# A hybrid attention and RWKV-7 block on one core: the tile scheduler orders instructions by its timeline simulation

## The chip, the cores and the metric

The kernel runs on one core of a Trainium2 chip. The metric is device time in microseconds (us), from the start to the end of one execution. The engines are named as in the profile: PE is TensorE (matmuls, with PEld its weight loads), DVE is VectorE, ACT is ScalarE, POOL is GpSimd, SP is SyncE, which issues the DMAs. "Profiled execution" is one run taken with the hardware profiler.

## The reference

One layer for 1024 tokens of width 1024, in float32. The parts that matter here, cut:

```python
h = rmsnorm(x, g_mix)
z = h @ w_in                       # columns: MLA latents | RWKV r,k,v,decay,a,g | two gates of 1024
o_mla  = mla_branch(z[MLA], ...)   # 8 heads, causal attention, blocks of 128 queries
o_rwkv = rwkv7_branch(z[RWKV], ...)
#   S_t = S_{t-1} diag(decay_t) + (S_{t-1} a_t) b_t^T + v_t k_t^T ;  y_t = S_t r_t
#   then a norm per head, bonus, output gate, @ w_o_rwkv
mix = sigmoid(gate0) * o_mla + sigmoid(gate1) * o_rwkv
x = x + mix @ w_out
hid = square(relu(rmsnorm(x, g_ffn) @ w_ffn_up))     # 1024 -> 4096
x = x + hid @ w_ffn_down                             # 4096 -> 1024
# then the gated per-layer embedding (ple) and the final rmsnorm
```

## The kernel before, in words

Activations are kept with the 1024 channels on partitions (eight tiles of 128) and the 1024 tokens along the free axis. Every dense product is written with its operands split in a high and a low part of type fp32r: `split_act` makes the high part as a cast on ACT and the low part as a difference on DVE (L318/L319 for activations, L215/L216 for weights), and three products are summed in a PSUM tile `psd` (L225: `xh*wh`, `xl*wh`, `xh*wl`), 48 matmuls of 128x512 for a block of 128 output channels.

The work around the change, in the order of the program:

- **Projections of the input** (`main`, a generator over all blocks of `w_in`): first the RWKV and MLA columns, then the two gates, 16 blocks. The gate blocks aren't needed before the merge, and the program uses them as filler: `weave` alternates the generator with other generators, one step of each in proportion to constants (`T_MAIN`, `T_EARLY`, `T_LATE`).
- **The RWKV recurrence in chunks of 64 tokens** (`recurrence`): 16 steps `chain(ci)`, a pair of steps for each group of 128 tokens. In each step PE, DVE and ACT alternate: products with the state `W` (L795, tile `pc`; L801, tile `py`), a copy `qs` (L797, DVE), a product with an inverse made earlier (L806), two copies into `W` (L807 DVE, L808 ACT), the products for the next state (L812) and the output (L820), the new state (L816, DVE), then the statistics of the output (L825 to L830). Two products are independent of the state: `vT` (L778) and `bk` (L784). `pre(g)` (L712 to L756) prepares the next group beside it, and `finish(g)` (L836 to L857) ends a group: a norm, transposes `yT` (L846), ACT and DVE operations and two stores. The last group's `finish`, behind the loop, is called the tail here.
- **Attention** (L1049 to L1100), by heads and blocks of 128 queries, beside projections of the latents (`qp`, `kn`, `v`).
- **Merge and output projection**, with the residual `res` (L1203).
- **The norm ahead of the FFN** (`row_sums_rstd`, L1207): column sums of squares on PE (L288, tile `st`), a short run of DVE operations, a scaled identity `dg` (L1215, DVE), its product with ones (L1220, tile `rb`, PE), a copy (L1221, ACT), and the scaling of `res` by `rb` (L1361, DVE). Beside it runs a product that nothing needs until the end: the ple projection, eight blocks of 12 matmuls (L1564).
- **FFN** in a Strassen-like form (L1338, tiles `psX`, `psY`, `psZ`), with operands `xb` and `sw` split on ACT and DVE (L318, L319) from `res` and its sums `bt` (L1385 to L1418).

The program runs under a tile framework. The code only gives each instruction, its operands and its place in the program; the framework's scheduler then chooses, from the instructions whose operands are ready, the order in which each engine's instructions are written, and puts in the semaphore waits. To choose, it needs a time for each candidate, and this comes from a model inside the framework. Each engine of the chip runs its list in the order so written.

## Time and profile before

| | before |
|---|---|
| median of 3 runs | 1784.69 us (1783.11 to 1784.8) |
| profiled execution | 1785.7 us, of which 1783.6 us span |
| mean granted PE clock | 0.991 of full speed |
| PE busy | 1730.2 us, 97% of the span |
| weight loads (PEld) busy | 1398.0 us, 78% |
| DVE busy | 1198.3 us, 67% |
| ACT busy | 834.8 us, 47% |
| POOL busy | 261.1 us, 15% |

The span runs from the first to the last instruction of the profiled execution. An engine's busy time is the time that its instructions took; times of PE and PEld overlap, since weights are loaded ahead. A granted clock of 1.00 is TensorE's higher level, 2.4 GHz, and 0.50 is 1.2 GHz.

### The profile page before, as it was taken

How to read it: one execution, taken by the hardware profiler on the slowest of the kernel's cores; microseconds unless marked ns; L12 is line 12 of the kernel's file. 1: busy time of each engine (PE TensorE's matmuls, PEld its weight loads, DVE VectorE, ACT ScalarE, POOL GpSimd, SP SyncE). 2: the span in 40 equal slices, each digit the busy share in tenths (PEclk: the TensorE clock that was granted, in tenths of full speed). 3: DMA queues.
4: the chain of work that ended last, by engine and by line, in shares of the span. 5: the costliest groups of instructions: out<-in, count | busy, mean ns of one | idle time of the engine just before them, and what ended most of it. 6: DMA issues, size and time to landing. Idle time of an engine off the chain costs nothing.

```text
span 1783.6 us, 26948 instructions
## 1 busy us (share of the span) xinstructions
PE 1730.2 (97%) x10525; PEld 1398.0 (78%) x10525; DVE 1198.3 (67%) x1882; ACT 834.8 (47%) x1409; POOL 261.1 (15%) x206
## 2 busy tenths in 40 slices
PE   7999999899999999999999999999999999999997
PEld 6877877777787867776887887888888888888886
DVE  6546695857777678888364369555668787787665
ACT  5553333234444365565344156555557344354444
POOL 2000000000000021212000203232323333332000
PEclk9999999999999999999999999999999999999999
DMA  6257674744543510014443334544558754451402
GB/s 196 71 204 215 195 204 113 188 131 120 155 123 101 182 44 24 24 60 155 140 121 128 95 142 131 166 141 143 166 176 260 243 169 149 154 182 48 154 13 95
DMA packets 245694, 246.13 MB, mean 138 GB/s; under 512 B 48729, under 2 KB 194752, under 8 KB 245568
## 3 DMA queue, kind: packets, MB, share of 16 engines
q1 hardware_dynamic: 243792, 239.65, 43.9%
q0 software_dynamic: 1760, 4.76, 0.8%
q8 instruction: 83, 1.36, 0.3%
q14 instruction: 43, 0.35, 0.1%
q10 hardware_dynamic: 16, 0.00, 0.0%
HBM read 162.31 MB, written 81.54 MB: 137 GB/s over the span
## 4 chain that ended last, share of the span: by engine, by line
PE 56%; DVE 5%; ACT 2%; issue 1%; POOL 0%; DMA 0%; DVEq 0%; ACTq 0%; POOLq 0%
PE psX L1338 18%; PE psd L225 12%; PE psY L1338 9%; PE psZ L1338 5%; PE po L1100 3%; PE pb L234 2%; PE pT L1087 1%; PE qp L234 1%; PE s L1057 1%; PE s L1059 1%; PE s L1058 1%; DVE xb L319 1%; DVE res L1361 1%; PE xT L1175 0%; DVE sw L319 0%
## 5 line engine op out<-in xcount | busy, mean ns | idle before, releaser
L1338 PE MATMUL psX<-xb,sw 128*128 128x512 f32 x768 | 177.4, 389 | 2.3 <-ACT hid L1441 1.2
L1338 PE MATMUL psX<-hb,sw 128*128 128x512 f32 x768 | 176.8, 389 | 0.0
L225 PE MATMUL psd<-xh,wh 128*128 128x512 f32 x528 | 172.8, 404 | 0.0
L225 PE MATMUL psd<-xl,wh 128*128 128x512 f32 x528 | 171.3, 402 | 0.0
L1338 PEld LDWEIGHTS psX<-xb,sw 128*128 128x128 f32 x768 | 144.0, 188 | 32.9 <-ACT hid L1441 1.6
L1338 PEld LDWEIGHTS psX<-hb,sw 128*128 128x128 f32 x768 | 144.2, 188 | 29.9
L225 PE MATMUL psd<-xh,wl 128*128 128x512 f32 x528 | 137.4, 399 | 0.0
L319 DVE TENSOR_TENSOR sw<-sw,sw 128x512 fp32r<-128x512 f32 x128 | 95.1, 747 | 58.2 <-ACT sw L318 58.0
L215 ACT CAST wh<-wr 128x1024 fp32r<-128x1024 f32 (+2 forms) x72 | 62.4, 869 | 152.3 <-PE psd L225 137.3
L318 ACT CAST sw<-sw 128x512 fp32r<-128x512 f32 x128 | 79.4, 620 | 102.1 <-PE psX L1338 37.0
L225 PEld LDWEIGHTS psd<-xh,wh 128*128 128x128 f32 x528 | 99.9, 192 | 22.3 <-issue 0.7
L225 PEld LDWEIGHTS psd<-xl,wh 128*128 128x128 f32 x528 | 100.0, 191 | 22.0
L225 PEld LDWEIGHTS psd<-xh,wl 128*128 128x128 f32 x528 | 97.3, 188 | 21.2
L216 DVE TENSOR_TENSOR wl<-wr,wh 128x1024 fp32r<-128x1024 f32 (+2 forms) x72 | 71.7, 997 | 60.9 <-PE psd L225 42.8
L318 ACT CAST sw<-wr 128x512 fp32r<-128x512 f32 x96 | 59.3, 622 | 71.5 <-PE psX L1338 39.3
L1338 PE MATMUL psY<-hb,sw 128*128 128x512 f32 x384 | 89.6, 389 | 0.0
L1338 PE MATMUL psY<-xb,sw 128*128 128x512 f32 x384 | 89.6, 389 | 0.0
L319 DVE TENSOR_TENSOR sw<-wr,sw 128x512 fp32r<-128x512 f32 x96 | 81.1, 845 | 12.6 <-ACT sw L318 12.4
L1338 PEld LDWEIGHTS psY<-hb,sw 128*128 128x128 f32 x384 | 72.1, 188 | 14.9
L1338 PEld LDWEIGHTS psY<-xb,sw 128*128 128x128 f32 x384 | 72.1, 188 | 14.9
L318 ACT CAST hb<-braw 128x1024 fp32r<-128x1024 f32 x56 | 58.7, 1048 | 52.2 <-DMA braw<-hid_d 20.1
L319 DVE TENSOR_TENSOR hb<-braw,hb 128x1024 fp32r<-128x1024 f32 x56 | 76.3, 1362 | 9.4 <-ACT hb L318 9.1
(409 smaller groups left out, 3546.8 us busy)
## 6 DMA issues: line engine op xcount, KB each, us to landing
hid_d<-hid SPq DMA_DIRECT2D x112, 256.0 KB, 4.3
braw<-hid_d SPq DMA_DIRECT2D x56, 512.0 KB, 4.4
wr<-in_w_in_dram SPq DMA_DIRECT2D x35, 512.0 KB, 5.3
wr<-in_w_ffn_up_dram SPq DMA_DIRECT2D x32, 512.0 KB, 5.0
wr<-in_w_ffn_down_dram SPq DMA_DIRECT2D x32, 512.0 KB, 4.3
gate_d<-gt SPq DMA_DIRECT2D x16, 512.0 KB, 3.7
gate<-gate_d SPq DMA_DIRECT2D x16, 512.0 KB, 3.7
xt<-in_x_dram SPq DMA_DIRECT2D x8, 512.0 KB, 8.4
```

The costliest lines, as they stand in the source:

```text
L215: A.copy(dst(wh), src)
L216: V.tensor_tensor(dst(wl), src, dst(wh).bitcast(F32), ALU.subtract)
L225: T.matmul(acc[:, h, :], lhsT=wt[:, k, :], rhs=r[k][:, h * 512:h * 512 + 512], start=wt is wh and k == 0 and ri == 0, stop=wt is wl and k ...
L234: T.matmul(acc, lhsT=wt[:, k, :], rhs=r[k][:, sl], start=wt is wh and k == 0 and ri == 0, stop=wt is wl and k == kb - 1)
L318: A.copy(hi, src)
L319: V.tensor_tensor(lo, src, hi.bitcast(F32), ALU.subtract)
L1057: T.matmul(sc[:, pi, :wc], lhsT=qh_[0:96, qs], rhs=kh_[0:96, ks], start=True, stop=False)
L1058: T.matmul(sc[:, pi, :wc], lhsT=qh_[0:96, qs], rhs=kl_[0:96, ks], start=False, stop=False)
L1059: T.matmul(sc[:, pi, :wc], lhsT=ql_[0:96, qs], rhs=kh_[0:96, ks], start=False, stop=not lastp)
L1087: T.transpose(out=tp_[:, b * P:(b + 1) * P], in_=prs[i][:, (4 * g + b) * P:(4 * g + b + 1) * P], identity=ident)
L1100: T.matmul(po[i * 64:i * 64 + 64, 0:P], lhsT=vt[kb // 2][:, kb % 2, h * 64:h * 64 + 64], rhs=pts[i][:, kb * P:(kb + 1) * P], start=kb == 0 ...
L1338: T.matmul(acc, lhsT=w[:, wl_, j, :], rhs=part(b, xl_, j), start=start and s == 0, stop=key == LAST[bank] and s == len(steps) - 1, skip_gr ...
```

## The change

The context in which the scheduler works is opened with another option. With `schedule_with_timeline_sim=True` the scheduler times candidate instructions with its timeline simulation in place of its default timing. Nothing else of the program is edited: the instructions, their shapes and their number on each engine are the same in both, and only their order (and with it the waits) differs.

```diff
-    with _tile.TileContext(nc) as tc:
+    with _tile.TileContext(nc, schedule_with_timeline_sim=True) as tc:
         tile_block(tc, *args)
```

The order on PE differs in many places. Three are shown. In all of them a name such as `psd_651_4674` is one tile, and `x8` stands for eight like instructions in a row.

**The recurrence on PE.** In the list of before, counted from the first L795 of one step to the first L795 of the next, the stretches ahead of step 0, between the steps and behind the start of step 15 hold these numbers of L225 matmuls: 1080 ahead of step 0, then 1, 7, 41, 0, 50, 0, 50, 0, 51, 0, 50, 0, 50, 0, 11 between the steps, and 1201 behind the start of step 15. With the change they are 1168 ahead, then 37, 35, 43, 40, 43, 36, 43, 41, 2, 0, 0, 0, 0, 0, 0, and 1104 behind. Step 10, the tile `pc_665`, is one of those that lose their filler; the list of PE before, from its first L795 on (`psd_651` is a gate block):

```order
L795 MATMUL pc_665_4767<-W_655_4716,q3_619_4471 64x64
L225 MATMUL psd_651_4674<-xh_11_165,wl_650_4671 128x512
L795 MATMUL pc_665_4767<-W_655_4716,q3_619_4471 64x64 x7
L225 MATMUL psd_651_4674<-xh_11_165,wl_650_4671 128x512
L225 MATMUL psd_651_4674<-xh_12_166,wl_650_4671 128x512
L801 MATMUL py_666_4768<-W_655_4716,q3_619_4471 64x64 x8
L806 MATMUL pc_665_4767<-qs_667_4777,mt1_1198 64x64 x8
L225 MATMUL psd_651_4674<-xh_12_166,wl_650_4671 128x512
L225 MATMUL psd_651_4674<-xh_13_167,wl_650_4671 128x512 x2
L225 MATMUL psd_651_4674<-xh_14_168,wl_650_4671 128x512 x2
L225 MATMUL psd_651_4674<-xh_15_169,wl_650_4671 128x512
L820 MATMUL py_666_4768<-W_655_4716,ar_637_4601 64x64
```

The same step with the change:

```order
L795 MATMUL pc_665_4767<-W_655_4716,q3_619_4471 64x64 x8
L736 MATMUL bo_677_4857<-r_671_4794,blkr_1192 128x128 x4
L806 MATMUL pc_665_4767<-qs_667_4777,mt1_1198 64x64 x8
L801 MATMUL py_666_4768<-W_655_4716,q3_619_4471 64x64 x8
L820 MATMUL py_666_4768<-W_655_4716,ar_637_4601 64x64
L812 MATMUL pc_665_4767<-W_655_4716,bk_663_4762 64x64 x8
L820 MATMUL py_666_4768<-W_655_4716,ar_637_4601 64x64 x7
L846 MATMUL yT_686_4894<-ident_92,yc_605_4415 64x64 x16
L752 MATMUL sc_692_4929<-q3_673_4796,sh_674_4797 128x128 x4
L801 MATMUL py_699_4971<-W_676_4840,q3_619_4471 64x64 x8
```

The dense matmuls between L795 and L806, and between L806 and L820, have gone; the blocks they belong to now stand ahead of step 9. The gate blocks that stood beside the last steps and the tail (`psd_752`, `psd_799`, `psd_809`) stand there too, and only `psd_837` and `psd_844` are still behind the transposes of the tail, `yT_810`.

**The norm ahead of the FFN on PE.** The list of before, around the column sums (`st`) and the product for `rb`:

```order
L288 MATMUL st_1687_9776<-ones_131,ssq_1650_9353 128x1 x8
L1564 MATMUL psd_1704_9839<-pl_1632_9250,pwh_1641_9286 128x512
...
L1564 MATMUL psd_1706_9855<-ph_1631_9249,pwl_1645_9293 128x512
L1220 MATMUL rb_1692_9797<-dg_1691_9795,ones_131 128x512
L1220 MATMUL rb_1693_9800<-dg_1691_9795,ones_131 128x512
```

With the change:

```order
L288 MATMUL st_1687_9776<-ones_131,ssq_1650_9353 128x1 x8
L1564 MATMUL psd_1708_9871<-ph_1630_9248,pwh_1641_9286 128x512 x2
...
L1564 MATMUL psd_1712_9903<-ph_1630_9248,pwl_1642_9287 128x512
L1220 MATMUL rb_1692_9797<-dg_1691_9795,ones_131 128x512
L1220 MATMUL rb_1693_9800<-dg_1691_9795,ones_131 128x512
```

Of the 96 matmuls of the ple projection, 17 stood ahead of the column sums before, and 36 do with the change; 35 stood ahead of the product for `rb`, and 69 do with the change.

**The first operands of the FFN on DVE.** Before, the scalings of `res` (L1361) alternate with the low parts of the first operands (L319, `xb`):

```order
L1361 SCALAR_TENSOR_TENSOR res_1502_8536<-res_1502_8536,pc_rest_134,rb_1686_9775 128x1024
L1361 SCALAR_TENSOR_TENSOR res_1504_8538<-res_1504_8538,pc_rest_134,rb_1686_9775 128x1024
L319 TENSOR_TENSOR xb_1720_9957<-res_1502_8536,xb_1718_9955 128x512
L1361 SCALAR_TENSOR_TENSOR res_1506_8540<-res_1506_8540,pc_rest_134,rb_1686_9775 128x1024
L319 TENSOR_TENSOR xb_1720_9957<-res_1504_8538,xb_1718_9955 128x512
```

With the change:

```order
L1361 SCALAR_TENSOR_TENSOR res_1502_8536<-res_1502_8536,pc_rest_134,rb_1686_9775 128x1024
L1361 SCALAR_TENSOR_TENSOR res_1504_8538<-res_1504_8538,pc_rest_134,rb_1686_9775 128x1024
L1361 SCALAR_TENSOR_TENSOR res_1506_8540<-res_1506_8540,pc_rest_134,rb_1686_9775 128x1024
...
L1361 SCALAR_TENSOR_TENSOR res_1509_8543<-res_1509_8543,pc_rest_134,rb_1686_9775 128x1024
L1385 TENSOR_TENSOR bt_1729_9984<-res_1502_8536 128x512
L319 TENSOR_TENSOR xb_1720_9957<-res_1502_8536,xb_1718_9955 128x512
```

All eight scalings now stand ahead of the first low part, where two did.

Elsewhere: the projections inside attention (`kn`, `qp`) are written some blocks earlier, with the same numbers of matmuls for each head; the two inverses made for the recurrence have 42 (first) and 83 (second) fewer dense matmuls ahead of the first product of their last stage (L684), and about 42 between each of the following pairs of products, where 1 to 3 stood for most; the FFN's list differs by swaps of neighbours; the last stage's is the same.

## Rows read from the trace of the kernel before

**Rows 1.** The page, busy time of each engine, share of the span, instructions

```profile
PE 1730.2 (97%) x10525; PEld 1398.0 (78%) x10525; DVE 1198.3 (67%) x1882; ACT 834.8 (47%) x1409; POOL 261.1 (15%) x206
```

**Rows 2.** By stretch: length, busy PE PEld DVE ACT POOL (instructions), PE clock, DMA share, GB/s

```profile
388.20:576.90 188.70, 188.34 (x2317) 149.66 (x2316) 142.05 (x332) 81.18 (x158) 0.00 (x0) 1.00 0.49 131
576.90:603.60 26.70, 26.70 (x195) 21.42 (x195) 11.83 (x24) 9.40 (x16) 0.00 (x0) 1.00 0.45 137
...
647.00:853.00 206.00, 197.07 (x1383) 147.03 (x1382) 167.44 (x382) 120.72 (x307) 40.92 (x36) 1.00 0.19 65
...
1063.50:1107.00 43.50, 41.25 (x181) 33.52 (x179) 41.97 (x52) 28.53 (x46) 12.52 (x7) 1.00 0.31 98
1107.00:1670.00 563.00, 562.99 (x2484) 466.33 (x2485) 387.80 (x484) 278.47 (x432) 173.85 (x112) 1.00 0.52 164
```

**Rows 3.** Waits of PE: line waited for, total us, times, longest

```profile
PE xT L376 <- DVE xt L370: 8.0, 2, 6.8
PE y L684 <- DVE x L677: 6.2, 1, 6.2
...
PE rT L293 <- DVE rr L207: 3.1, 1, 3.1
...
PE L L640 <- DVE a L632: 2.2, 2, 1.3
```

**Rows 4.** Stretches in the recurrence, and behind two gaps of PE

```profile
388.20:403.40 15.20, 15.12 (x235) 12.21 (x234) 12.70 (x31) 5.25 (x13) 0.00 (x0) 1.00 0.64 171
506.28:511.74 5.46, 5.46 (x102) 4.78 (x101) 3.59 (x9) 2.01 (x5) 0.00 (x0) 1.00 1.00 284
506.28:533.94 27.66, 27.66 (x324) 21.99 (x323) 20.48 (x47) 12.49 (x24) 0.00 (x0) 1.00 0.55 145
237.50:244.20 6.70, 6.70 (x43) 4.93 (x44) 6.67 (x9) 0.74 (x2) 0.00 (x0) 0.50 0.23 54
353.40:360.20 6.80, 3.14 (x11) 2.50 (x12) 2.47 (x2) 2.99 (x3) 0.00 (x0) 0.50 0.92 175
```

**Rows 5.** Two of these stretches and the tail, the dense matmuls of L225 alone

```profile
388.20:403.40 15.20, 2.92 (x8) 1.32 (x8) 1.00 0.64 171
506.28:533.94 27.66, 13.92 (x50) 8.84 (x50) 1.00 0.55 145
576.85:603.58 26.73, 23.30 (x98) 18.08 (x98) 1.00 0.45 137
```

**Rows 6.** Critical chain, around the output projection: start, us, piece

```profile
955.45 82.10 PE psd L225 x362
```

**Rows 7.** Timeline of step 15 and the tail: start, us, instruction

```profile
576.85 0.75 PE L795 MATMUL pc<-W,q 128*64 128x64 f32 x16
...
578.07 1.23 DVE L216 TENSOR_TENSOR wl<-wr,wh 128x1024 fp32r<-128x1024 f32 x1
...
586.77 0.69 DVE L839 TENSOR_TENSOR yc<-yc,rr 128x512 f32<-128x512 f32 x1
...
593.30 1.15 PE L846 MATMUL yT<-ident,yc 64*64 64x64 f32 x32
...
603.58 0.62 PE L225 MATMUL psd<-xh,wh 128*128 128x512 f32 x2
```

**Rows 8.** Timeline around the norm ahead of the FFN

```profile
1037.38 1.07 PE L1564 MATMUL psd<-ph,pwh 128*128 128x512 f32 x4
...
1041.91 1.95 PE L288 MATMUL st<-ones,ssq 128*128 128x1 f32 x16 [0.52 <-DVE ssq L313]
...
1047.93 1.88 PE L1220 MATMUL rb<-dg,ones 128*128 128x512 f32 x4
...
1050.46 2.48 DVE L1361 SCALAR_TENSOR_TENSOR res<-res,pc_rest,rb 128x1024 f32<-128x1024 f32 x2 [3.86 <-ACT rb L1221]
...
1052.86 0.68 DVE L319 TENSOR_TENSOR xb<-res,xb 128x512 fp32r<-128x512 f32 x1
...
1063.50 2.88 PE L1338 MATMUL psX<-xb,sw 128*128 128x512 f32 x12
```

## The prediction

> **What bounds the kernel now.** I read the page first, then busy times by stretch, the waits of PE, and the timeline in three places. PE works 1730.2 of 1783.6 us [rows 1], so only 53.4 us are idle, and a new order can win no more than that plus what a low clock costs; it can lose much more, by taking cover from a chain of dependent work. By stretch [rows 2] the reader is to see which engine stands behind PE. In the FFN (1107 to 1670) PE is busy 562.99 of 563.00 us: no order of neighbours changes that. In the recurrence (388.2 to 576.9) PE is also full, 188.34 of 188.70, but with a mixture: by the counts of the order 311 dense matmuls lie between its steps, and 98 more beside the tail [rows 5]. Between the norm and the full FFN (1063.5 to 1107) DVE is the nearest to full, 41.97 of 43.5 us. Attention has some slack on all engines. The waits of PE [rows 3] are few and early: 8.0 us for the first transposes, 6.2 for the second inverse, 3.1 and 2.2 for the norms of the recurrence. The only stretches at the low clock that matter lie behind two of these waits [rows 4], the two stretches at 0.50.
>
> **The change, part by part.** Instructions and durations stay; a dense matmul that moves from one full stretch of PE to another is free. So I price only the places that lose or gain cover.
>
> *A. The recurrence.* The order takes away the 151 dense matmuls that stood between steps 8 and 14, the 11 ahead of step 15, and those beside the tail up to `psd_837`. What was covered is read from one pair of steps: 27.66 us from step 9 to step 11, of which 50 matmuls are dense [rows 4, 5]. A dense matmul takes 82.10/362 = 0.2268 us on PE when they follow each other [rows 6]; so dense work is 11.3 us of the pair, and PE's own work there 27.66 - 11.3 = 16.3 us. If PE bounded a bare pair, it would take 16.3 us and the move would be free. It won't: DVE works 20.48 us in the pair, of which one weight split of 1.23 us (L216) [rows 7] belongs to the dense block, which leaves 19.3 us. So 19.3 is the lower bound of a bare pair. Three rows say that DVE won't reach it: in the half without dense work, 506.28 to 511.74, DVE is busy 3.59 of 5.46 us, 1.87 idle, and two such dependent halves give 19.3 + 2 x 1.87 = 23.0; the first pair, with only 8 dense matmuls, has DVE busy 12.70 of 15.20, 84%, and 19.3/0.84 is 23.0 again [rows 4]. The steps are a dependent chain through three engines, but with the order free of dense rows DVE can run `pre` and `finish` in the holes; I take 22. Each bare pair then costs 22 - 16.3 = 5.7 us over the free case, three pairs 17 us (bounds 9 from 19.3, 20 from 23.0). Step 14 has 11 dense matmuls and no `pre` beside it; I put its loss at nothing, between 0 and the 2.5 us that they take.
>
> The tail: from the L795 of step 15 at 576.85 to the next block `psd_837` at 603.58 [rows 7] are 26.73 us, with 98 dense matmuls = 22.2 us [rows 5], so 4.5 us are PE's own. The chain in it ends on DVE at 586.77 + 0.69 = 587.46, 10.6 us after the L795; the transposes could have run then, but stood behind a dense block until 593.30. With the cover gone ahead of step 9, the tail costs 10.6 + 1.15 = 11.8 us before PE has dense work again, against 4.5: +7.3. Bounds: 5, if the DVE work that goes with the dense blocks (1.23 us twice) delayed the chain before, and 8. **A = 17 + 7 = +24 us** (14 to 30).
>
> *B. The norm ahead of the FFN.* 34 more matmuls of the ple projection stand ahead of the product for `rb` (69 against 35): 34 x 0.2268 = 7.7 us later on PE. It ran at 1047.93 [rows 8], so now at about 1055.6. The scaling on DVE waits for it (it began at 1050.46), and from there to 1107 DVE is the bound (96% of the stretch behind 1063.5), so what it starts later it ends later. Then eight scalings of 1.24 us stand ahead of the first low part in place of two, which delays the first FFN product: 1050.46 + 7.7 + 8 x 1.24 + 0.69 + 0.68 = 1069.5 against 1063.50, with PE idle in between, for the ple projection is used up by 1063.5. This lies inside the delay of DVE's list, so it isn't added. **B = +8 us**; from 3, if PE's own 41.25 us in the stretch show that DVE's list had reserve, to 10.
>
> *C. The inverses.* Fewer dense matmuls stand ahead of their last stage, so the waits of 3.1 and 6.2 us stay or grow; against that, about 42 stand between the products that ran nearly bare, part of it at clock 0.50. If all three waits went, 6.2 + 3.1 + 2.2 = 11.5 us, and the two slow stretches (6.70 and 3.14 us of PE at half speed, 4.9 us to win). I take the two as about equal: **C = +2** (-10 to +12; the upper end is 42 x 0.2268 = 9.5 us less cover, plus the next wait).
>
> *D. The start.* A weight split and a statistic stand ahead of the first two activations on DVE; one such split is 1.23 us [rows 7]. The first transposes come about 2 us later, the later ones earlier. **D = +1** (-2 to +4).
>
> *E. Attention, merge, FFN.* In attention PE is busy 197.07 of 206.00 us [rows 2], 8.9 idle, and the same filler is written a block earlier. Nothing at 0 (-4 to +6); the FFN is full on PE and its list nearly the same, 0.
>
> Sum: 24 + 8 + 2 + 1 = **+35** on the profiled execution's 1785.7, 1820.7 us; the median shown is 1.0 us lower than the profiled execution, so **1819.5 us**.
>
> **The rivals.** *The clock falls in the bare steps.* With 22 us for 16.3 of PE, PE waits some 3 us in each step, in pieces. Behind a single wait of 3.1 and one of 6.2 us the granted clock was 0.50 for 6.7 and 6.8 us [rows 3, 4]. Against it: in attention PE idles 8.9 us in many pieces and the clock stays at 1.00 [rows 2], and the first pair, nearly bare, has 1.00 [rows 4]. The price: PE's own work from step 8 to the tail is 3 x 16.3 + about 13 + 4.5 = 66 us; at half speed throughout 132, against some 91 available, so +41; for most of it +30, and the time is about **1850**. In the Trainium skill ("TensorE: Matmul & The Clock Gate", Part 1: The HAM clock gate) the throttled state is the default, and it is activity that releases it; by that rule the bare steps are the ones at risk, and the two rows at 0.50 agree with it, while the attention row shows that short pieces of idleness don't suffice. I leave this case one chance in ten.
>
> *Not slower: the filler was worth more early than late.* The 88 dense matmuls that now stand ahead of step 0 lie where PE waited, and the bare steps fill PE by themselves. For it: in the first pair PE was busy 15.12 of 15.20 us with 8 dense matmuls [rows 4]. Against it: that pair has no `finish` beside it, and DVE has 19.3 us in a later one. Price: the early waits and slow stretches give 11.5 + 4.9 = 16.4 us, the pairs cost nothing, the tail 7 and B at its lower bound 3: 1785.7 + 10 - 16.4 - 1.0 = about **1778**. It decides from the point where a bare pair takes under about 17 us.
>
> *Only the norm and the tail cost.* Pairs at DVE's 19.3, or early gains of about 10 us: 1785.7 + 9 + 7 + 5 - 8 - 1 = about **1798**, mildly slower.
>
> *Nothing measurable.* The order differs almost everywhere, so "no change" could come only as a balance of the above, within about 3.6 us.
>
> **How the numbers follow.** A difference of 0.2%, 3.6 us, is about what a measurement of this kernel can tell from no change. Chances: the forecast, slower by 20 to 50 us, 0.60; mildly slower (4 to 20 us), 0.17; clock in the bare steps, 0.10; balance, 0.06; faster, 0.07. So slower 0.87, same 0.06, faster 0.07. The likeliest is 1819.5. The range from 1796 to 1845 takes in the mildly slower case from its middle on and the bounds of the sum (A 14, B 3, C 0, D 0 give 1802; A 30, B 10, C 12, D 4 give 1841), and leaves out the balance, the faster case and most of the case of the clock.
>
> **What would show it.** In the trace of the changed kernel: (A) pairs of steps from step 8 on at 21 to 23 us with DVE busy over 85% and PE under 80%, the early pairs at 33 us or more with PE full, and about 12 us from the last L795 to `psd_837`; (B) `rb` about 8 us later relative to the first ple matmul, a hole of 5 us or more on PE ahead of the first `psX`, and the FFN full from about 8 us later; (C) waits of PE at L684 and L293 as long as before or longer. A shows wrong if the bare pairs run at 17 us with PE full, or at a clock of 0.50; B, if PE fills before DVE's list is through; the whole, if the early stretches give back over 15 us.

## The result: 4.45% slower, outside the forecast range

| | before | with the change |
|---|---|---|
| median | 1783.9 us (1781.41 to 1784.8, 4 runs) | 1863.33 us (1862.19 to 1867.39, 4 runs) |
| profiled execution, span | 1785.7, 1783.6 us | 1863.51, 1861.8 us |
| mean granted PE clock | 0.991 | 0.963 |
| PE idle in the span | 53.4 us | 108.3 us |

The ratio is 1.0445 (95% interval 1.043 to 1.0459). The sign was forecast; the size wasn't: +35 us forecast, +79 measured. The page of the changed kernel shows where to look; these are the row of busy times [rows 1] and two of the rows by slices of 1/40 of the span (46.5 us each):

```profile
PE 1753.5 (94%) x10525; PEld 1431.6 (77%) x10525; DVE 1208.9 (65%) x1882; ACT 834.0 (45%) x1409; POOL 260.6 (14%) x206
...
PE   5999999999997778998899998999999999999998
...
PEclk9999999899996699999999999999999999999998
```

PE's idle time has doubled (1861.8 - 1753.5 = 108.3 us), and PE is busy 23 us longer with the same instructions, because part of them ran at a lower clock: the 13th and 14th slice (558 to 652 us), 7 tenths busy, stand at 6 tenths of the clock. This is the second half of the recurrence.

To put the loss in its places I compare when the same matmul starts in both traces, and take off what only changed sides: a dense matmul more ahead of it counts 0.2268 us [rows 6]. What is left is called the net delay; the last column is its growth from the row above. The product of step 0, for instance, starts 28.9 us later but has 88 dense matmuls more ahead of it (1168 against 1080), so its net delay is 28.9 - 88 x 0.2268 = 9.0 us.

| first matmul of | before, us (dense ahead) | after, us (dense ahead) | net delay | forecast for the piece | measured |
|---|---|---|---|---|---|
| transposes, L376 | 9.7 (0) | 13.7 (0) | 4.0 | D +1 | +4.0 |
| step 0, L795 | 388.2 (1080) | 417.1 (1168) | 9.0 | C +2 | +5.0 |
| step 9 | 506.3 (1280) | 562.9 (1488) | 9.5 | A 0 | +0.5 |
| step 15 | 576.9 (1391) | 649.8 (1488) | 50.9 | A +17 | +41.4 |
| last `yT`, L846 | 593.3 (1448) | 659.2 (1488) | 56.8 | A +7 | +5.9 |
| first scores, L1057 | 646.3 (1584) | 712.5 (1584) | 66.2 | none | +9.4 |
| merge, L1175 | 851.1 | 921.8 | 70.8 | E 0 | +4.6 |
| `rb`, L1220 (34 ple matmuls more ahead) | 1047.9 | 1123.4 | 67.8 | | -3.0 |
| 13th `psX`, L1338 | 1066.2 | 1141.3 | 75.1 | B +8 | +7.3 |
| last transposes, L1637 | 1760.2 | 1838.6 | 78.5 | 0 | +3.4 |

More than half is one piece, steps 9 to 15. The steps there and a filled one ahead of them, by stretch from one step's first product to the next (columns as in [rows 2]):

```profile
501.67:518.82 17.15, 17.15 (x165) 13.64 (x164) 10.99 (x22) 6.33 (x12) 0.00 (x0) 1.00 0.45 124
562.93:575.04 12.11, 6.79 (x121) 5.63 (x121) 8.48 (x21) 5.92 (x12) 0.00 (x0) 0.89 0.98 237
575.04:596.77 21.73, 16.87 (x172) 14.59 (x172) 14.87 (x35) 5.55 (x12) 0.00 (x0) 0.50 0.08 23
596.77:612.26 15.49, 11.86 (x109) 10.22 (x109) 9.09 (x17) 4.91 (x9) 0.00 (x0) 0.50 0.53 142
612.26:628.46 16.20, 11.66 (x164) 10.01 (x164) 11.08 (x30) 5.55 (x12) 0.00 (x0) 0.71 0.11 30
628.46:637.58 9.12, 8.69 (x102) 7.75 (x101) 3.39 (x9) 2.18 (x5) 0.00 (x0) 0.52 0.23 65
637.58:649.75 12.17, 7.75 (x148) 6.73 (x148) 8.78 (x25) 4.04 (x12) 0.00 (x0) 0.86 0.01 2
```

The first row is a filled step: PE full at 1.00. Then the filler is gone (the next two rows are the pair that took 27.66 us before with 50 dense matmuls [rows 4]; now 12.11 + 21.73 = 33.8 us with none), and the granted clock is 0.50 to 0.89. The same steps 9 to 15 in one row, before and with the change:

```profile
506.28:576.85 70.57, 70.29 (x904) 55.86 (x903) 52.42 (x127) 31.03 (x62) 0.00 (x0) 1.00 0.47 124
562.93:649.75 86.82, 63.63 (x812) 54.93 (x812) 55.69 (x134) 28.15 (x62) 0.00 (x0) 0.65 0.30 77
```

Before, 111 of the matmuls are dense, 25.2 us by the price above, so PE's own work was 45.1 us. With the change there are none, and PE is busy 63.6 us: 18.5 us more, of which about 1 us is work that changed sides (812 matmuls against 904 - 111 = 793). PE waits 23.2 us where it waited 0.3. So the 41.4 us are about 18 us of the same work at a lower clock and 23 us of waits.

The clock fell here, in the timeline around step 9 (start, us, instruction, idle ahead of it and its releaser):

```profile
566.76 0.65 SPq L716 DMA_DIRECT2D r<-rkv_d  x1
...
573.43 0.69 DVE L732 TENSOR_TENSOR q<-r,e 128x512 f32<-128x512 f32 x1 [2.21 <-DMA r<-rkv_d]
574.04 0.85 DVE L816 TENSOR_TENSOR W<-pc,dt 64x256 f32<-64x256 f32 x2
...
575.04 1.12 PE L795 MATMUL pc<-W,q 128*64 128x64 f32 x16 [3.69 <-DVE W L816]
```

The state update (L816), for which the next step's product waits, stands on DVE behind the preparation of the next group (L732), and that waits 2.21 us for its load of `r`, issued at 566.76. PE waits 3.69 us in one piece; before it PE had worked in pieces, 6.79 us of the 12.11 in the step; from here on the rows show 0.50.

The tail and what follows, in the same view:

```profile
649.75 0.69 PE L795 MATMUL pc<-W,q 128*64 128x64 f32 x16
...
659.18 1.97 PE L846 MATMUL yT<-ident,yc 64*64 64x64 f32 x32 [4.95 <-DVE yc L839]
...
661.08 1.22 PE L225 MATMUL psd<-xh,wh 128*128 128x512 f32 x2
...
712.50 0.28 PE L1057 MATMUL s<-kh,q 96*128 96x256 f32 x1
```

From the last step's product to the next dense matmul are 11.3 us (11.8 forecast). But from the last `yT` to the first scores are 53.3 us, and before they were 646.3 - 593.3 = 53.0, although 136 dense matmuls lay in them before (1584 - 1448) and now 96. Before, and with the change:

```profile
593.30:646.29 52.99, 50.38 (x247) 41.05 (x247) 39.41 (x50) 27.53 (x45) 7.57 (x8) 1.00 0.52 161
659.18:712.50 53.32, 46.50 (x207) 37.19 (x207) 37.82 (x48) 26.02 (x44) 7.73 (x8) 0.89 0.42 135
```

Without the 40 dense matmuls (9.1 us) PE had 50.4 - 9.1 = 41.3 us of work here. It took 46.5 at a clock of 0.89, 5.2 us more, and PE waits 6.8 us in place of 2.6, 4.2 more: together the 9.4 us of the table. In the other runs below the same stretch is 52.3 to 54.8 us, with 96 to 136 dense matmuls in it.

Around the norm [rows 8]:

```profile
1114.14 1.84 PE L288 MATMUL st<-ones,ssq 128*128 128x1 f32 x16
...
1123.41 1.88 PE L1220 MATMUL rb<-dg,ones 128*128 128x512 f32 x4
...
1125.95 9.66 DVE L1361 SCALAR_TENSOR_TENSOR res<-res,pc_rest,rb 128x1024 f32<-128x1024 f32 x8 [6.78 <-ACT rb L1221]
...
1131.28 0.61 PE L1338 MATMUL psX<-xb,sw 128*128 128x512 f32 x2
...
1136.13 0.68 DVE L319 TENSOR_TENSOR xb<-res,xb 128x512 fp32r<-128x512 f32 x1
...
1136.87 3.78 PE L1338 MATMUL psX<-xb,sw 128*128 128x512 f32 x8 [4.97 <-DVE xb L319]
```

PE has nothing ready from 1131.9 to 1136.87 (two products of `psX` ran on the high parts, the third needs the low part that stands behind eight scalings of 9.66 us in all). The long waits of PE over the whole execution [rows 3]:

```profile
PE xT L376 <- DVE xt L370: 11.1, 1, 11.1
PE yT L846 <- DVE yc L839: 8.2, 3, 5.0
PE y L684 <- DVE x L677: 6.2, 3, 4.6
...
PE st L288 <- DVE ssq L539: 3.6, 1, 3.6
...
PE psd L225 <- DVE pg L1594: 1.9, 1, 1.9
```

The start waits 11.1 us where it waited 8.0; the inverse waits 6.2 in three pieces; a wait for a sum of squares (L539, ahead of the recurrence) of 3.6 us is new; and one of 1.9 us in the last stage.

### The profile page after: what moved, and what is told of

It reads as the page before. It is cut to its first block, busy times and chain, and to the rows that moved or that the text cites. A ratio compares the mean times of both kernels' runs of the same rounds, so it can differ in the third digit from the quotient of the medians.

```text
span 1861.8 us, 27023 instructions
## 1 busy us (share of the span) xinstructions
PE 1753.5 (94%) x10525; PEld 1431.6 (77%) x10525; DVE 1208.9 (65%) x1882; ACT 834.0 (45%) x1409; POOL 260.6 (14%) x206
## 4 chain that ended last, share of the span: by engine, by line
PE 56%; DVE 6%; ACT 2%; issue 1%; DMA 1%; DVEq 0%; ACTq 0%; SPq 0%
PE psX L1338 18%; PE psd L225 12%; PE psY L1338 9%; PE psZ L1338 5%; PE pb L234 2%; PE po L1100 2%; PE qp L234 1%; PE pT L1087 1%; DVE nmx L1063 1%; PE psd L1564 1%; PE s L1057 1%; PE s L1059 1%; PE s L1058 1%; DMA latf<-lat_d 1%; DVE prob L1070 1%
## 5 line engine op out<-in xcount | busy, mean ns | idle before, releaser
L1338 PE MATMUL psX<-xb,sw 128*128 128x512 f32 x768 | 181.6, 393 | 5.9 <-DVE xb L319 5.2
L1338 PE MATMUL psX<-hb,sw 128*128 128x512 f32 x768 | 180.3, 389 | 0.0
L1338 PEld LDWEIGHTS psX<-xb,sw 128*128 128x128 f32 x768 | 145.5, 190 | 37.5 <-DVE xb L319 6.1
L225 PE MATMUL psd<-xh,wh 128*128 128x512 f32 x528 | 171.8, 405 | 0.0
L225 PE MATMUL psd<-xl,wh 128*128 128x512 f32 x528 | 171.2, 402 | 0.0
L1338 PEld LDWEIGHTS psX<-hb,sw 128*128 128x128 f32 x768 | 144.1, 188 | 29.9
L225 PE MATMUL psd<-xh,wl 128*128 128x512 f32 x528 | 135.2, 401 | 0.0
L319 DVE TENSOR_TENSOR sw<-sw,sw 128x512 fp32r<-128x512 f32 x128 | 96.1, 752 | 55.8 <-ACT sw L318 55.6
L225 PEld LDWEIGHTS psd<-xl,wh 128*128 128x128 f32 x528 | 101.1, 193 | 22.4
L225 PEld LDWEIGHTS psd<-xh,wh 128*128 128x128 f32 x528 | 100.8, 194 | 21.9 <-issue 0.4
L225 PEld LDWEIGHTS psd<-xh,wl 128*128 128x128 f32 x528 | 99.0, 191 | 21.8
L319 DVE TENSOR_TENSOR sw<-wr,sw 128x512 fp32r<-128x512 f32 x96 | 91.8, 967 | 12.4 <-ACT sw L318 11.0
L1338 PE MATMUL psY<-hb,sw 128*128 128x512 f32 x384 | 92.7, 389 | 0.0
L1338 PE MATMUL psY<-xb,sw 128*128 128x512 f32 x384 | 91.5, 390 | 0.0
L1338 PEld LDWEIGHTS psY<-xb,sw 128*128 128x128 f32 x384 | 72.4, 188 | 15.1
L1502 DVE TENSOR_TENSOR res<-psX,res 128x512 f32<-128x512 f32 x64 | 44.0, 688 | 60.9 <-PE psX L1338 59.0
L1338 PEld LDWEIGHTS psY<-hb,sw 128*128 128x128 f32 x384 | 72.1, 188 | 15.0
```

What stands on the lines that cost most here:

```text
L225: T.matmul(acc[:, h, :], lhsT=wt[:, k, :], rhs=r[k][:, h * 512:h * 512 + 512], start=wt is wh and k == 0 and ri == 0, stop=wt is wl and k ...
L319: V.tensor_tensor(lo, src, hi.bitcast(F32), ALU.subtract)
L1338: T.matmul(acc, lhsT=w[:, wl_, j, :], rhs=part(b, xl_, j), start=start and s == 0, stop=key == LAST[bank] and s == len(steps) - 1, skip_gr ...
L1502: V.tensor_tensor(dst, acc, dst, ALU.add)
```

## The experiments

All ratios are to the kernel before, run on the same chip beside the experiment. The theory after the result: the filler that left the last steps is the cause, and it costs twice, by the chain's own latency at full clock (which the forecast had) and by the low clock that the bare steps bring about. Two rivals: the option's fine order on DVE is needed for the loss (the load wait above); or the low clock only goes along with latencies that would be there anyway. In most of the kernels edges hold an instruction behind another on the same engine in the order that is written, with no wait: `behind(ins, key)` below, where `mark[key]` is the earlier one.

**1. Option on, filler held back.**

```diff
-  T.matmul(acc[:, h, :], lhsT=wt[:, k, :], ...)                 # L225, dense
+  behind(T.matmul(acc[:, h, :], lhsT=wt[:, k, :], ...), "step")
-  T.matmul(pc_[LOH[h], 0, j, :], ...)                           # L795 of a step
+  mark["step"] = T.matmul(pc_[LOH[h], 0, j, :], ...)
```

> The option stays on, and each dense matmul (L225) of the recurrence's stretch is written behind the first product (L795) of the step that the program traces ahead of it, so 16 to 32 of them lie in every gap between steps. If the pulled-forward filler is the cause (A), the 41 us lost between steps 9 and 15, the 6 of the tail and the 9 up to the first scores go: about 1863 - 56 = 1807 us, clock near 1.00 through the recurrence. Rival: the loss lies in the fine order of the steps themselves (DVE's list, the transposes), which stays: 1835 or more.

Measured 1836.86 us, ratio 1.0304 (1.0285 to 1.0323): 26.5 us back, of the 56 expected. The net delay grows from 13.4 at step 0 to 33.0 at step 15, evenly, in place of 9.0 to 50.9. In the steps, 19.6 us are left of 41.9, so holding the filler back wins more than half of the loss there and a third of the whole, and the rival's bound of 1835 is met: something else costs some 20 us in the steps. Two of them, of 12.13 and 17.52 us:

```profile
491.19:503.32 12.13, 11.76 (x135) 9.12 (x135) 9.38 (x20) 5.97 (x12) 0.00 (x0) 1.00 0.96 283
503.32:520.84 17.52, 17.20 (x205) 13.99 (x205) 12.86 (x32) 6.82 (x14) 0.00 (x0) 1.00 0.01 4
```

PE is nearly full, and the clock is 1.00 in these two; in the next two (520.84 to 554.98) it is 0.92 and 0.88. What the 20 us are, run 6 tells apart in part.

**2. Option off, filler forward.** The mirror image: the program of before, with the gate blocks handed out early.

```diff
-  run(weave([(recurrence(), T_LATE), (main, T_MAIN)], lead=True))
+  run(until(main, 19)); run(weave([(recurrence(), T_LATE), (until(main, 75), 800)]))
```

> The option is off, as before, but the program hands out the gate blocks of the recurrence early, so that steps 7 to 15 stand bare (3 dense matmuls in all). If bare steps by themselves cost the time (low clock included), this is slower than before by 40 to 55 us: 1825 to 1840. Rival: the option's order of DVE, in which the preparation of the next group stands ahead of the state update and waits for its loads, is needed for the loss; then about +20 at a clock of 1.00: 1800 to 1808.

Measured 1843.17 us, ratio 1.0343 (1.0326 to 1.036), 61 us slower than before and 3 us above the upper end of the first expectation. Net delays: -4.0 at step 8, 39.6 at step 15 (43.6 us in the bare steps), 45.2 at the last `yT`, 55.7 at the first scores, and nothing behind it (55.3 at the end). So a loss of A's size appears without the option and without its order on DVE. Over steps 9 to 15 alone (559.70 to 638.48), this run is busy on PE for 63.55 of 78.78 us, as long as the changed kernel (63.63), and waits 15.2 us where that waits 23.2: the longer PE work is the same without the option, and 8 us of waits go with the option's order. From step 6 to step 12 of it:

```profile
511.18:532.44 21.26, 21.26 (x219) 16.45 (x218) 17.00 (x39) 10.92 (x20) 0.00 (x0) 1.00 0.39 99
532.44:537.90 5.46, 5.46 (x101) 4.78 (x100) 3.58 (x9) 1.40 (x4) 0.00 (x0) 1.00 1.07 302
537.90:559.70 21.80, 14.46 (x173) 12.34 (x172) 16.16 (x38) 8.00 (x17) 0.00 (x0) 0.67 0.31 68
559.70:570.12 10.42, 10.42 (x104) 8.94 (x105) 5.08 (x13) 2.35 (x6) 0.00 (x0) 0.55 0.72 200
570.12:589.34 19.22, 12.59 (x169) 11.12 (x168) 14.36 (x34) 7.95 (x17) 0.00 (x0) 0.74 0.15 44
589.34:600.22 10.88, 10.88 (x104) 9.35 (x105) 5.51 (x14) 2.56 (x6) 0.00 (x0) 0.51 0.78 215
```

The first row is filled, the second the short half behind it, without dense matmuls, at a clock of 1.00: 5.46 us. The third is the first bare long half, PE busy 14.46 of 21.80, and the clock falls within it. From there each short half takes 10.4 to 10.9 us, with PE full, in place of 5.46: at half the clock twice the time. A bare pair takes 29.6 us (10.42 + 19.22).

**3. Option on, filler forward, state update first.** To test whether the load wait of 3.7 us starts the fall.

```diff
-  V.scalar_tensor_tensor(a, a, -1.0, cbc("k_a"), ...)           # L726, of the next group
+  behind(V.scalar_tensor_tensor(a, a, -1.0, cbc("k_a"), ...), "state")
-  V.tensor_tensor(q3[:, 2], c8(r), c8(e1), ALU.mult)            # L732
+  behind(V.tensor_tensor(q3[:, 2], c8(r), c8(e1), ALU.mult), "state")
-  V.tensor_tensor(Wn[R, h], pc_[R, 0], dt[R], ALU.add)          # L816
+  mark["state"] = V.tensor_tensor(Wn[R, h], pc_[R, 0], dt[R], ALU.add)
```

The dense matmuls also have edges that let them run eight steps ahead at most, so that steps 9 to 15 are bare as in the changed kernel.

> The option stays on and the filler stays forward (steps 8 to 15 bare), but on DVE the preparation of the next group (L726 on) is written behind the latest state update (L816), so the chain no longer stands behind work that waits for loads. If that wait of 3.7 us dropped the clock and started the loss, the clock stays at 1.00 in the bare steps and they cost what was forecast (22 us a pair): about 1863 - 22 = 1840. Rival: bare steps run at the low clock in any case: 1855 to 1868.

Measured 1893.71 us, ratio 1.0629 (1.0612 to 1.0645): slower than either expectation. A bare pair of it:

```profile
601.51:626.55 25.04, 12.87 (x173) 11.01 (x173) 16.70 (x38) 7.44 (x16) 0.00 (x0) 0.72 0.29 67
626.55:636.72 10.17, 9.32 (x102) 8.21 (x101) 3.41 (x9) 4.90 (x9) 0.00 (x0) 0.51 0.86 225
```

25.04 + 10.17 = 35.2 us at 0.72 and 0.51. The preparation, pushed back, now arrives late itself: PE waits 16.3 us in four pieces for L733 of the preparation. So taking the chain from behind the loads doesn't keep the clock, and with run 2, where no such order exists, the theory that this wait is needed falls. The edge also changed where filler stands in steps 0 to 8, so the price of that wait by itself stays open.

**4. Option on, norm and start put back.**

```diff
-  T.matmul(acc[:, h, :], lhsT=wt[k][:, cs], ...)                # L1564, ple projection
+  behind(T.matmul(acc[:, h, :], lhsT=wt[k][:, cs], ...), "rb" if m >= 3 else "")
-  T.matmul(pt, lhsT=ones, rhs=dg[:, hs], ...)                   # L1220
+  mark["rb"] = T.matmul(pt, lhsT=ones, rhs=dg[:, hs], ...)
-  V.tensor_scalar(xts[tb], xts[tb], r[:, tb % 2:tb % 2 + 1], None, ALU.mult)    # L370
+  mark["xt"] = V.tensor_scalar(xts[tb], xts[tb], r[:, tb % 2:tb % 2 + 1], None, ALU.mult)
-  V.scalar_tensor_tensor(junk, xts[tb], 1.0, ...)               # L365
+  behind(V.scalar_tensor_tensor(junk, xts[tb], 1.0, ...), "xt")
-  V.tensor_tensor(dst(wl), src, ...)                            # L216
+  behind(V.tensor_tensor(dst(wl), src, ...), "xt")
```

> The option stays on; only two places are put back: at most 36 matmuls of the ple projection stand ahead of the product for rb (69 with the change, 35 before), and at the start the scalings of the first tokens (L370) stand ahead of the weight splits and of the second statistic. By B the norm gives back 7 us and by D the start 4: about 1852. Rival: what is won at either place is lost again behind it, 1860 to 1866.

Measured 1853.07 us, ratio 1.0392 (1.0375 to 1.041): 10.3 us back, as expected. The first transposes start at 10.7 us (13.7 with the change, 9.7 before). Around the norm:

```profile
1105.37 1.84 PE L288 MATMUL st<-ones,ssq 128*128 128x1 f32 x16
...
1110.46 3.78 PE L1220 MATMUL rb<-dg,ones 128*128 128x512 f32 x4 [3.25 <-DVE dg L1215]
...
1128.63 5.60 PE L1338 MATMUL psX<-xb,sw 128*128 128x512 f32 x24
```

`rb` now waits for DVE, 1110.46 - 1105.37 = 5.1 us behind the column sums (9.3 with the change, 6.0 before), and the first products of `psX` run without a hole. But the 10 us don't come from the two places as expected. From the first matmul of the merge to the 13th `psX` this run takes 218.28 us, where the change takes 219.45 and the kernel before 215.15: at the norm 1.2 us are won and not 7, for what `rb` gains is mostly lost ahead of it. Step 0 stands at a net delay of -1.3 in place of 9.0: 3.0 of these 10.3 us are won at the first transposes, 7.3 behind them. Then 5.8 us are lost again up to step 9, and 7.8 won in steps 9 to 15. That the total fits the expectation is luck.

**5. Option off, filler forward, unread matmuls in every bare step.** To hold the clock: from step 8 on, four 128x512 matmuls behind each of three products of a step, into a PSUM tile that nobody reads.

```diff
+  jk = psd(s="jk") if ci >= 8 else None
+  fillin = lambda jk: [behind(T.matmul(jk[:, 0, :], lhsT=xh[0][:, 0:P], rhs=xh[1][:, 0:512], start=True, stop=True), "jk")
+                       for _ in range(4 if jk is not None else 0)]
```

> The kernel of the second run (option off, filler forward, bare from step 7 or 8 on) with extra dense matmuls whose result nobody reads: from step 8 on, four each behind the first, second and third product of a step, 12 a step or 2.7 us, 22 us in all. If the low clock makes the bare steps long (29 to 30 us a pair at a clock of 0.54 and 0.75), the extra work keeps the clock at 1.00 and the pairs come down to 22 or 23 us: the kernel is faster than the second run in spite of more work, by 15 to 25 us, about 1822. Rival: the chain's latencies set the pair and the clock only goes along; then the pairs stay at 29 or more and the time at 1843 or above.

Measured 1856.98 us, ratio 1.0399 (1.0383 to 1.0414): slower than run 2, by the rival's side. But the clock wasn't held:

```profile
543.64:563.83 20.19, 15.68 (x182) 13.07 (x181) 14.19 (x33) 7.86 (x17) 0.00 (x0) 0.74 0.12 34
563.83:576.19 12.36, 12.36 (x116) 9.33 (x116) 5.40 (x13) 4.99 (x10) 0.00 (x0) 0.73 0.72 203
607.27:624.08 16.81, 12.68 (x182) 10.05 (x181) 13.93 (x35) 5.37 (x13) 0.00 (x0) 1.00 0.04 11
```

The tile of the extra matmuls took a buffer from a gate block, which moved beside the tail, so the steps were bare two earlier, without extra matmuls, and the clock had already fallen there. It stayed at 0.52 to 0.80 until 607 us, and the short halves became longer by the extra work (12.36 us). Only the third row shows what was asked for: a long half at 1.00 with 12 extra matmuls takes 16.81 us, against 19.0 to 19.2 without them at 0.74 to 0.76 in run 2. Inconclusive as a whole; it led to run 8.

**6. Option off, filler even.** The edges of run 1 on the kernel before.

> The same edges as in the first run (each dense matmul behind the first product of the step traced ahead of it, 16 to 32 a step), but with the option off. If the first run's remaining 20 us in the recurrence come from the option's fine order of the steps on DVE, this one is as fast as before, 1784 to 1790. Rival: they come from the even spread, which covers the long half of a pair too little and the short half too much; then about 1800 to 1806.

Measured 1803.11 us, ratio 1.0105 (1.0089 to 1.0122), 18 us slower than before, a small loss but clear of the noise: the rival's number. Its places: 6.4 us are there at step 0 already (68 dense matmuls fewer ahead of it; the waits there lost cover), 9.8 come evenly in steps 0 to 15, and 1.4 behind them (17.6 at the end). A long and a short half:

```profile
491.58:509.83 18.25, 18.07 (x205) 13.90 (x205) 13.74 (x32) 11.18 (x20) 0.00 (x0) 1.00 0.25 57
509.83:520.88 11.05, 10.99 (x134) 8.58 (x133) 8.36 (x19) 3.31 (x7) 0.00 (x0) 1.00 1.05 283
```

With the same edges and the same counts of dense matmuls (24, 24, 32, 20, ...), the option on costs 19.6 us in the steps and off 9.8; and behind the recurrence, on: 6.2 up to the scores, 9.2 in attention, 3.8 from the merge to the 13th `psX`; off: 1.4 in all. So of run 1's rest in the steps half is the even spread, and about 10 us go with the option's own order of the steps. On which engine's list they lie is not settled; part of them may be the clock, which stood at 0.92 and 0.88 in two of run 1's steps and at 1.00 here from step 5 on.

**7. Option on, everything put back** (edges of 1 and 4).

> Option on, with the edges of the first and of the fourth run together. If the terms add, 1837 - 11 = 1826 us, still 2.4% slower than before. Rival: the early places move again once the start is earlier, 1835 or more.

Measured 1834.76 us, ratio 1.0279 (1.0262 to 1.0296): at the rival's bound of 1835, 2 us below run 1 in place of 11. The start is won (a net delay of 1.1 us at the first transposes, 4.0 in run 1), but at step 0 the delay is 13.6 as in run 1 (13.4): what the start gave is gone by then, whereas in run 4 it grew. From the merge to the 13th `psX` 1.3 us are won.

**8. Option off, filler forward, unread matmuls only in the long halves.** As 5, but from step 6 on, in even steps only, six behind each of L795, L806, L812 and L820: 24 in a long half, 5.4 us.

```diff
+  jk = psd(s="jk") if ci >= 6 and c == 0 else None
```

> As the fifth run, but the unread matmuls stand only in the long half of each pair (even steps from 6 on), where PE waits, 24 in each (6 behind each of four products, 5.4 us), and from before the place where the clock fell. If the bare pair is latency of the chain (5.5 + at most 16.8 us at a clock of 1.00) plus a surcharge of the low clock, PE's waits are filled, the clock stays at 1.00 through the recurrence, the short halves come back to 5.5 us (10.4 to 11.2 in the second run) and a pair takes 23 to 25 us in place of 29.7, with 5.4 us more PE work in it: 1825 to 1835. Rival: pairs of 29 us or more, the short halves staying above 10, and 1843 or more; then the low clock isn't what makes the bare pairs longer than forecast.

Measured 1839.4 us (1833.15 to 1851.46), ratio 1.0319 (1.027 to 1.0368): between the bounds, and the least steady of all kernels here. Its own trace holds both cases, in order of time:

```profile
504.35:509.81 5.46, 5.46 (x101) 4.78 (x100) 3.59 (x9) 1.40 (x4) 0.00 (x0) 1.00 1.05 298
509.81:528.33 18.52, 16.25 (x194) 12.58 (x193) 16.19 (x37) 10.20 (x19) 0.00 (x0) 1.00 0.44 110
528.33:534.89 6.56, 6.34 (x104) 5.38 (x104) 4.68 (x12) 2.35 (x6) 0.00 (x0) 1.00 0.85 237
534.89:551.48 16.59, 15.57 (x194) 12.40 (x193) 14.71 (x37) 6.62 (x16) 0.00 (x0) 1.00 0.43 83
551.48:558.00 6.52, 6.33 (x104) 5.37 (x104) 4.65 (x12) 2.35 (x6) 0.00 (x0) 1.00 0.81 224
558.00:578.18 20.18, 16.90 (x194) 13.54 (x193) 15.33 (x37) 8.01 (x17) 0.00 (x0) 0.89 0.31 72
578.18:589.30 11.12, 11.12 (x104) 9.43 (x104) 5.75 (x14) 2.64 (x6) 0.00 (x0) 0.50 0.74 204
589.30:609.79 20.49, 17.53 (x193) 14.54 (x192) 13.97 (x32) 7.72 (x16) 0.00 (x0) 0.83 0.07 19
```

Up to 558 us the clock is 1.00, and the pair from 528.33 takes 6.56 + 16.59 = 23.15 us, 24 extra matmuls included; the one ahead of it 5.46 + 18.52 = 23.98. In the next long half the clock falls, although PE is busy 16.90 of 20.18 us, and from there the pair is 11.12 + 20.49 = 31.6 us with the same instructions. So in one execution, with the same PE instructions in the pair, a pair takes 31.6 - 23.15 = 8.5 us longer at the low clock. Of these, 6.7 us are PE's own busy time (28.65 against 21.91), so the low clock doesn't only go along. Which came first can be seen too: from 568 to 572 us, still at 1.00, PE was busy 1.51 of 4.00 us, in gaps of 1.3 us at most, and from 574 us on the clock stood at 0.50. That the extra matmuls hold the clock reliably is not shown: with them it stayed up for four steps.

## Why the prediction was wrong

**The step that failed is the premise under A, "Instructions and durations stay".** The instructions stayed, the durations didn't. Over steps 9 to 15 PE is busy about 18 us longer for the same work, at a mean granted clock of 0.65, and behind the tail 5.2 us longer, at 0.89; the two make up nearly all of the 23.3 us by which PE's busy time grew over the whole execution (1753.5 - 1730.2). The sum has no term for that. The waits, which it does have, were nearer: 17 us forecast for the bare steps; 15.2 us of waits in run 2, and 23.2 with the change, whose order holds the state update behind loads (3.7 us in one piece). At full clock, run 8 has pairs of 23.15 and 23.98 us, with 5.4 us of extra matmuls in them, close to the 22 of the text; at the low one a pair takes 29.6 us (run 2), 31.6 (run 8), and 33.8 and 31.7 with the change.

**A was also counted wrong.** It has three bare pairs and nothing for step 14. But by the order shown with the change, 41 and 2 dense matmuls are left between steps 7 and 9, and this pair cost 0.5 us. Two pairs were bare, steps 9 to 11 and 11 to 13, at 17.5 and 15.4 us over the free case of 16.3, and steps 13 to 15 cost the other 8.5.

**The rival that happened was the first one, with a chance of 0.10.** Its mechanism was right, and so was its place; it priced the low clock at +30 us, and PE's busy time grew by 23.3. The argument against it was the error: attention with 8.9 us of idle pieces at a clock of 1.00, and the nearly bare first pair at 1.00. In the first pair PE was busy 15.12 of 15.20 us, so it says nothing of a step with waits; and attention has PE at 197.07 of 206.00 us [rows 2], whereas the long half in which the clock fell has it at 14.46 of 21.80 (run 2). The Trainium skill ("TensorE: Matmul & The Clock Gate", Part 1: The HAM clock gate) says that the throttled state is the default and that activity releases it. By that rule the bare steps were at risk, and the trace agrees on the fall: 0.50 to 0.89 there, 1.00 in the filled steps ahead of them. On the return it agrees only in part: in runs 2 and 8 short halves in which PE had no gap ran at 0.50 to 0.55, and there the measurement decides.

**A place was left out: ahead of attention, +9.4.** The tail was priced to the next dense block and no further (7 forecast, 5.9 measured). The text said that a dense matmul moved from one full stretch to another is free, and it didn't ask about the stretch behind the tail, which lost 40 of them. It kept its length of 53 us: 4.2 us more of waits and 5.2 us more of PE's time at the lower clock fill what the 40 left. In run 1, with 106 dense matmuls there and a clock of 0.97, it is 52.3 us, so the clock alone doesn't set it; whether a chain of attention's operands does is not shown.

**B had the mechanism, but was too large**: +8 forecast, +7.3 measured between `rb` and the 13th `psX`, with a hole of 5.0 us ahead of the third product. But the -3.0 ahead of `rb` belongs to it, for it is gone (+0.3) in runs 4 and 7, where the ple projection was put back. From the merge to the 13th `psX`, with all 96 ple matmuls inside in both traces, the change costs 75.1 - 70.8 = 4.3 us, and run 4 won 1.2 of them.

**C and D were mis-sized, D to the edge of its bounds**: +5.0 for +2, +4.0 for +1. **E**, priced at nothing, cost 4.6 in attention, and the last stage, also at nothing, 3.4. Together they are 17 us, where 3 were forecast. Why is not shown for each. The early places depend on each other: what was won at the start had grown to 10.3 us by step 0 in run 4 and was gone by step 0 in run 7.

**A slip in the sum**: 1820.7 - 1.0 is 1819.7, not 1819.5. It changes nothing else.

**The faster rival** needed bare pairs under about 17 us; they took 23 at full clock (run 8). No version here beats the kernel before: its own order with 50 dense matmuls in every long half and none in the short ones is faster than the even spread (run 6, 1.0105), the forward one (run 2, 1.0343) and all orders with the option.

## What to carry to other kernels

Before a cover is moved, ask three things of each place that loses it: how long the bare chain takes at the full clock, what it takes if the waits that open in it bring the low one (23 and 31.6 us a pair here), and which waits further on the moved work also covered. In this kernel, bound by PE, independent matmuls were worth most beside the chain in which PE waits; moved to where PE was full anyway they gained nothing. That a scheduler times the instructions in more detail is no evidence of a better order, as here: compare the two orders by what stands between the links of the chain, and price each gap from the trace.

## What the runs showed of the hardware that was not expected

In a chain of dependent steps the low clock, once there, stayed for most of the steps that followed. A short half of 101 to 105 matmuls takes 5.46 us with PE full at 1.00 and 10.4 to 11.1 us with PE full at 0.50 to 0.55, and the long half behind it brings the clock back only in part (0.74 to 0.83 on average in runs 2 and 8). In run 8 the clock fell in a half in which PE was busy 16.90 of 20.18 us and never waited longer than 1.3 us at a time, and full short halves (11.12 of 11.12 us) then ran at 0.50 from end to end. The four executions of run 8 spread over 18 us, where those of the kernel before spread over 6.
